# Emission by prioritised threads in a two-part transformer kernel: attention by head group, new orders of heads and projections, first recurrence blocks by token tile

## The chip, the cores and the metric

One core of one Trainium2 chip. The metric is the device time of one execution in microseconds; lower is better. Times of the kernel before: 2118.86 us, the median of 3 runs (2118.59 to 2119.57).

## What is computed

256 tokens of width 1024 pass through two models, one after the other, in float32.

```python
# first model: 4 layers, each
x = layer_norm(ALPHA * x + mixer(x))        # swa_sink, rglru, mla, swa_sink
x = layer_norm(ALPHA * x + memory_cross_attention(x))   # 4 heads of 256
x = layer_norm(ALPHA * x + conv_glu_ffn(x))             # d_ff 2816
# second model: 2 layers, each with rms_norm ahead of its parts
x = x + concat(local_heads(12 x 64), memory_heads(4 x 64)) @ w_out
x = x + conv_glu_ffn(x)
```

The mixers are: windowed attention with sinks (16 heads of 64, 4 key heads), in layers 0 and 3; a gated linear recurrence (rglru: input projection, convolution over time, two gates from 256-wide blocks, a scan over the tokens, a GELU gate, an output projection), in layer 1; latent attention (mla: down projection, norms, 8 heads of 128 + 64 rotary), in layer 2. The mixing layers of the second model are a forget-gate attention (fox) and a dilated attention, each with memory heads beside the local ones.

## The kernel before

The tokens are two tiles of 128 (t0 and t1). Every dense product is made in three matmuls of split operands: mm3 (lines 87, 88, 89) adds hi by hi, hi by lo and lo by hi, where hi is the rounded half of an operand and lo the rest. Weights come by DMA (raw, issued by SP); ScalarE casts hi (line 76) and VectorE subtracts lo (line 81), in wslot (line 66). While help_every is set, GpSimd makes each fifth lo in VectorE's place; rglru sets it, and it is reset after rglru's output projection b_w_o. The rings hold 6 raw tiles and 9 pairs of halves.

Activations are kept twice: X by rows (token on the partition), and a transposed, split pair xh, xl (or oh, ol for attention's output) that TensorE reads. The rows are turned by transposes with the identity (line 161). PSUM has three kinds of banks: four common ones (tag r) and two for each token tile.

project (line 179) runs one dense product for t0, then t1, and after each tile calls post, which takes the banks on: for the layer norm (line 227) that is VectorE's additions, statistics and scaling (lines 235 to 243), a power on GpSimd (line 224), then the transposes of X. Program text is emitted in that order, and a scheduler of the framework then orders each engine's queue by that order and by its own estimates; nobody writes a queue by hand.

attend (line 279) is called once for each token tile, when all its queries are there: it takes the heads in groups, scores (mask by identity at line 291, products at 296 and 301), the softmax (reduce 309, exp 316, scaling 325), turn (transposes of the probabilities pr, line 335, evacuated as pT), values (products with the values, line 355). It emits group i's scores, then group i-2's values, then group i-1's transposes. swa (line 431) projects keys and values, then queries of heads 0 to 7, then of 8 to 15, each for both tiles. mix (line 852) projects the forget gate and memory queries, keys, values, queries; it runs the main heads, then the memory heads of each tile.

rglru (line 477) first runs the softplus of its decay, then the gate projections gx of both tiles (transposed at 563), then conv_u (510) and gates (529) for four pairs of blocks, the transposed gate blocks (gate_bank, 560; gate_out, 573), and `late` blocks (588) whose gate projections stand near the end: late(4), gates(3), four gate_out, late(5) to late(7), four gate_out. Then b_w_o, its layer norm, and cross (line 394). There kh and kl split the memory keys (lines 400 and 401; kl on GpSimd), x_w_q projects the queries, and x_w_o the output. ffn (line 699) alternates up and down products; its order is not touched but for the lead of its first blocks.

## Time and profile before

| what | us |
|---|---|
| median of 3 runs | 2118.86 |
| the profiled execution, its own time | 2114.15 |
| its span | 2112.4 |
| TensorE busy (PE), 13528 matmuls | 2071.3 |
| VectorE busy (DVE) | 1613.5 |
| ScalarE busy (ACT) | 1218.4 |
| GpSimd busy (POOL) | 84.3 |

A window's row gives for a stretch of the span each engine's busy time and instructions, and the mean clock that was granted to TensorE (1.00 is full). A timeline's row gives start, busy time, engine, line, operation, out<-in and the number of instructions drawn together; in brackets stands how long the engine stood idle before it and what released it. Matmuls are pipelined, so a busy time is longer than the distance from one start to the next.

### The profile page before, as it was taken

How to read it: one execution, taken by the hardware profiler on the slowest of the kernel's cores; microseconds unless marked ns; L12 is line 12 of the kernel's file. 1: busy time of each engine (PE TensorE's matmuls, PEld its weight loads, DVE VectorE, ACT ScalarE, POOL GpSimd, SP SyncE). 2: the span in 40 equal slices, each digit the busy share in tenths (PEclk: the TensorE clock that was granted, in tenths of full speed). 3: DMA queues.
4: the chain of work that ended last, by engine and by line, in shares of the span. 5: the costliest groups of instructions: out<-in, count | busy, mean ns of one | idle time of the engine just before them, and what ended most of it. 6: DMA issues, size and time to landing. Idle time of an engine off the chain costs nothing.

```text
span 2112.4 us, 36195 instructions
## 1 busy us (share of the span) xinstructions
PE 2071.3 (98%) x13528; PEld 1853.0 (88%) x13528; DVE 1613.5 (76%) x3344; ACT 1218.4 (58%) x2654; POOL 84.3 (4%) x77
## 2 busy tenths in 40 slices
PE   8999999999999999999999999999999999999998
PEld 8778999887899987889997789998979998978997
DVE  6876877899787786787788778788568877677775
ACT  5545656585465554555555456665556665456563
POOL 0010000123000001000000100000000000000000
PEclk9999999999999999999999999999999999999999
DMA  8523655535455452555544347554426655524551
GB/s 331 183 94 124 228 186 183 176 102 213 168 200 187 150 188 80 180 183 192 186 152 168 120 138 251 191 179 155 160 85 220 206 182 167 183 81 170 200 180 61
DMA packets 101409, 358.23 MB, mean 170 GB/s; under 512 B 11888, under 2 KB 13552, under 8 KB 99312
## 3 DMA queue, kind: packets, MB, share of 16 engines
q1 hardware_dynamic: 101232, 355.91, 48.8%
q8 instruction: 106, 1.74, 0.3%
q14 instruction: 71, 0.58, 0.1%
HBM read 354.81 MB, written 1.05 MB: 168 GB/s over the span
## 4 chain that ended last, share of the span: by engine, by line
PE 89%; DVE 5%; ACT 3%; issue 1%; POOL 1%; DMA 1%; POOLq 0%; DVEq 0%; SPq 0%; ACTq 0%
PE bank L87 26%; PE bank L88 26%; PE bank L89 26%; PE bank L355 3%; PE bank L161 3%; DVE lo L81 2%; PE bank L335 2%; PE bank L301 1%; PE bank L296 1%; ACT pr L316 1%; ACT hi L76 1%; PE bank L291 1%; DMA row<-in_mem 0%; PE bank L769 0%; DVE nm L309 0%
## 5 line engine op out<-in xcount | busy, mean ns | idle before, releaser
L76 ACT CAST hi<-raw 128x512 fp32r<-128x512 f32 (+3 forms) x1300 | 745.9, 606 | 483.7 <-PE bank L89 222.5
L81 DVE TENSOR_TENSOR lo<-raw,hi 128x512 fp32r<-128x512 f32 (+3 forms) x1289 | 840.2, 673 | 182.3 <-ACT hi L76 177.6
L87 PE MATMUL bank<-xh,hi 128*128 128x256 f32 x1920 | 543.7, 283 | 0.0
L89 PE MATMUL bank<-xh,lo 128*128 128x256 f32 x1920 | 543.2, 283 | 0.0
L88 PE MATMUL bank<-xl,hi 128*128 128x256 f32 x1920 | 543.2, 283 | 0.0
L87 PEld LDWEIGHTS bank<-xh,hi 128*128 128x128 f32 x1920 | 368.5, 192 | 3.2 <-issue 0.2
L88 PEld LDWEIGHTS bank<-xl,hi 128*128 128x128 f32 x1920 | 368.2, 192 | 2.8
L89 PEld LDWEIGHTS bank<-xh,lo 128*128 128x128 f32 x1920 | 368.2, 192 | 0.5
L87 PE MATMUL bank<-hi,xh 128*128 128x256 f32 (+4 forms) x784 | 263.2, 336 | 0.2
L723 DVE SCALAR_TENSOR_TENSOR c<-bank,cw,c 128x254 f32<-128x254 f32 (+1 forms) x528 | 238.6, 476 | 32.1 <-ACT c L719 31.6
L89 PE MATMUL bank<-hi,xl 128*128 128x256 f32 (+4 forms) x784 | 262.1, 335 | 0.0
L88 PE MATMUL bank<-lo,xh 128*128 128x256 f32 (+4 forms) x784 | 260.4, 332 | 0.0
L87 PE MATMUL bank<-hi,gh 128*128 128x512 f32 x528 | 208.0, 394 | 0.7 <-ACT gh L92 0.7
L88 PE MATMUL bank<-lo,gh 128*128 128x512 f32 x528 | 206.9, 392 | 0.0
L89 PE MATMUL bank<-hi,gl 128*128 128x512 f32 x528 | 205.5, 390 | 0.0
L87 PEld LDWEIGHTS bank<-hi,xh 128*128 128x128 f32 x784 | 148.8, 190 | 12.0 <-ACT row L62 1.4
L89 PEld LDWEIGHTS bank<-hi,xl 128*128 128x128 f32 x784 | 148.7, 190 | 10.2 <-issue 1.0
L88 PE MATMUL bank<-lo,oh 128*128 128x512 f32 (+1 forms) x392 | 154.6, 395 | 2.8 <-DVE lo L81 1.8
L88 PEld LDWEIGHTS bank<-lo,xh 128*128 128x128 f32 x784 | 148.8, 190 | 9.3 <-issue 0.2
L87 PE MATMUL bank<-hi,oh 128*128 128x512 f32 (+1 forms) x392 | 154.4, 397 | 0.0
L89 PE MATMUL bank<-hi,ol 128*128 128x512 f32 (+1 forms) x392 | 152.7, 391 | 0.0
L719 ACT ACTIVATE c<-bank,cw 128x256 f32<-128x256 f32 x264 | 133.5, 559 | 0.2 <-PE bank L89 0.2
(270 smaller groups left out, 2570.1 us busy)
## 6 DMA issues: line engine op xcount, KB each, us to landing
raw<-in_f_w_up SPq DMA_DIRECT2D x176, 512.0 KB, 3.8
raw<-in_f_w_down SPq DMA_DIRECT2D x88, 512.0 KB, 3.8
raw<-in_m_w_up SPq DMA_DIRECT2D x88, 512.0 KB, 3.8
raw<-in_m_w_down SPq DMA_DIRECT2D x44, 512.0 KB, 3.5
raw<-in_m_w_qkv SPq DMA_DIRECT2D x48, 384.0 KB, 3.7
raw<-in_x_w_q SPq DMA_DIRECT2D x32, 512.0 KB, 3.5
raw<-in_x_w_o SPq DMA_DIRECT2D x32, 512.0 KB, 4.7
gb<-in_ln_gb SPq DMA_DIRECT2D x12, 1024.0 KB, 4.8
```

The source lines that it names most:

```text
L76: S.copy(hi[:, c], raw[:, c])
L81: eng.tensor_tensor(lo[:, c], raw[:, c], hi[:, c], ALU.subtract)
L87: T.matmul(ps, ah, bh, start=first, stop=False)
L88: T.matmul(ps, ah, bl, start=False, stop=False)
L89: T.matmul(ps, al, bh, start=False, stop=last)
L161: T.transpose(ps[:w, j * P : (j + 1) * P], b, ident)
L291: T.matmul(banks[b], l, r, start=(j == 0), stop=False)
L296: T.matmul(banks[b][:, i], l, r, start=(j == 0), stop=(j == len(pairs) - 1))
L335: T.transpose(tp[:, tile_cols(j)], prv[:, h % 2, h // 2, tile_cols(kt)], ident)
L355: T.matmul(po[i * w : (i + 1) * w, tile_cols(c - c0)], value(h0 + h, kt)[:, off : off + w], pT[h, kt], start=(kt == 0), stop=(kt == nk - 1),)
L719: S.activation(c[:, h], ps[:, h], AF.Identity, scale=cw[:, 2, b : b + 1], bias=cw[:, 3, b : b + 1])
L723: V.scalar_tensor_tensor(c[:, h, s:], ps[:, h, : 256 - s], cw[:, 2 - s, b : b + 1], c[:, h, s:], ALU.mult, ALU.add)
```

## The change

A generator (Thread) holds each piece of work, with a priority. `run` resumes the first thread in order of priority whose condition holds; a clock that is advanced by written-in costs (109 ns for a transpose, columns / 2.4 + 13.5 ns for a matmul) decides when a piece that waits for other engines may go on. So the program's text order is made by this emission, and the scheduler orders the queues from it. With it come these edits:

- project becomes `dense`, one thread for a tile, with weights that are loaded when first used (Rows); a post may yield for some microseconds before its transposes. The transposes of X go in two halves of four.
- attend makes one thread per head group; a group's scores start when its own inputs are there. swa projects in the order keys t0, first queries t0, keys t1, second queries t0, first queries t1, second queries t1, and heads 0 to 7 start when the first queries are there. mix runs the memory heads first and projects keys, queries, values.
- rglru: the two first convolution blocks are computed by token tile between the gate projections; the second late block stands ahead of gates(3); the softplus and its load move to load_constants.
- the output projections only start threads (out_proj), so that cross emits kh and kl ahead of b_w_o's weights; help_every stays set until the next ffn.
- the mask table loses a part, the latent keys' weights are laid out as four loads, and the layer norm's gains are loaded when its projection begins.

```diff
+    def run(*until, fed=False):
+        while not all(t is None or t.done or fed and t.fed for t in until):
+            soonest = None
+            for th in sorted(live, key=lambda t: t.prio):
+                r = th.when()
+                if r is None:
+                    continue
+                if r <= clk[0]:
+                    resume(th)
+                    break
+                soonest = r if soonest is None else min(r, soonest)
+            else:
+                assert soonest is not None
+                clk[0] = soonest
...
+    def transpose_rows(x, t, wait):
+        for h in range(2):
+            yield clk[0] + wait if h == 0 else again
+            again = clk[0] + 1500
+            if t == 0 and h == 0:
+                fresh("x")
+            c = slice(4 * h, 4 * h + 4)
+            transpose_split(col_blocks(x)[c], [d[:, c] for d in cur["x"]], t)
...
+    def out_proj(w, post, *heads):
+        ws = load_rows(w, D, 1)
+        for t in range(NT):
+            rows_of[t] = dense(
+                "o", ws, HALVES, t, post, need=after(*(heads[t] if heads else ())), lag=1300,
+                first=getattr(post, "prepare", None) if t == 0 else None,
+            )
...
+            yield from transpose_rows(X[:, t], t, 7500)
...
-        todo = list(range(0, heads, size))
-        made, turned = [], []
-        for i in range(len(todo) + 2):
-            if i < len(todo):
-                made.append(scores(todo[i]))
-            if i >= 2:
-                values(*turned.pop(0))
-            if 1 <= i <= len(todo):
-                turned.append(turn(*made.pop(0)))
+        def group(i, h0):
...
+            made = scores(h0)
+            recs[i].scored = clk[0]
+            turned = yield from turn(free, *made)
+            recs[i].turned = True
+            yield from values(*turned)
+            recs[i].done = True
...
+            jobs = [(0, 2, kvpost), (0, 0, qpost(0)), (1, 2, kvpost), (0, 1, qpost(1)), (1, 0, qpost(0)), (1, 1, qpost(1))]
...
+            def lead(t):
+                for a in range(2):
+                    if t == 0:
+                        ub.append((next(blocks), bank()))
+                    (hi, lo), ps = ub[a]
+                    xth, xtl = cur["x"]
+                    for k in range(KD):
+                        x = tile_cols(t)
+                        mm3(ps[:, x], hi[:, k], lo[:, k], xth[:, k, x], xtl[:, k, x], k == 0, k == KD - 1)
+                        yield
...
             late(ng)
+            late(ng + 1)
             gates(3, *prev)
             for c in range(ng):
                 gate_out(c, gz[:, c])
-            for c in range(ng + 1, KD):
+            for c in range(ng + 2, KD):
                 late(c)
...
-        project_full(cur["o"], A["b_w_o"], post)
-        help_every[0] = 0
+        out_proj(A["b_w_o"], post)
...
+            help_every[0] = 0
+            pinned[0] = "f"
+            run(*[spawn(lead(t), need=r) for t, r in enumerate(rows_ready())])
...
-            for w, f in ((1, kpost), (2, vpost), (0, qpost)):
-                project(cur["x"], load_rows(A["m_w_qkv"][l, w], 768, 1), halves, f)
+            for w, f in ((1, kpost), (0, qpost), (2, vpost)):
+                ws = load_rows(A["m_w_qkv"][l, w], 768, 1)
```

In the first local attention, TensorE's order before, from the first group's transposes of probabilities (ident,pr) to the products with the values (pT,vv); hi,xl, hi,xh and lo,xh are projections:

```order
L335 MATMUL bank<-ident,pr 128x128 x2
L87 MATMUL bank<-hi,xh 128x512
L88 MATMUL bank<-lo,xh 128x512
L335 MATMUL bank<-ident,pr 128x128 x3
L89 MATMUL bank<-hi,xl 128x512
L335 MATMUL bank<-ident,pr 128x128
L355 MATMUL bank<-pT,vv 64x128 x8
L335 MATMUL bank<-ident,pr 128x128 x8
L355 MATMUL bank<-pT,vv 64x128 x8
```

And the same place after the change, from the second four transposes of that group on:

```order
L532 MATMUL bank<-ident,pr 128x128 x4
L161 MATMUL bank<-hi,xh 128x512
L162 MATMUL bank<-lo,xh 128x512
L163 MATMUL bank<-hi,xl 128x512
L266 MATMUL bank<-ident,q 128x128 x4
L560 MATMUL bank<-pT,vv 64x128 x8
L161 MATMUL bank<-hi,xh 128x512
L162 MATMUL bank<-lo,xh 128x512
L163 MATMUL bank<-hi,xl 128x512
L481 MATMUL bank<-maskh,identr 128x512 x2
L491 MATMUL bank<-kT,qT 128x128 x8
```

Before, the transposes and products of two groups followed each other with three projection matmuls among them; now three matmuls and four transposes of q stand between a group's transposes and its products, and the next group's scores come after.

At the recurrence's entry, TensorE's order before (ident,X are the layer norm's transposes, ident,gx those of the first gate projection):

```order
L88 MATMUL bank<-lo,xh 128x512
L89 MATMUL bank<-hi,xl 128x512
L161 MATMUL bank<-ident,X 128x128 x4
L563 MATMUL bank<-ident,gx 128x128 x2
L161 MATMUL bank<-ident,X 128x128 x4
L87 MATMUL bank<-hi,xh 128x512
```

And now (xh,hi of 128x128 are the first convolution blocks for tile t0):

```order
L163 MATMUL bank<-xh,lo 128x128
L161 MATMUL bank<-xh,hi 128x128
L162 MATMUL bank<-xl,hi 128x128
L163 MATMUL bank<-xh,lo 128x128
L266 MATMUL bank<-ident,X 128x128 x4
L161 MATMUL bank<-xh,hi 128x128
L162 MATMUL bank<-xl,hi 128x128
L163 MATMUL bank<-xh,lo 128x128
```

33 such matmuls stand before the first four transposes of X, and 15 between these and the second four; the transposes of gx have moved behind t1's blocks.

GpSimd's queue from the recurrence to the layer norm behind the cross attention, before (gz belongs to the gates, lo to weights, kl to the memory keys, rs is the power of a norm):

```order
L81 TENSOR_TENSOR lo<-raw,hi 128x512 x5
L574 TENSOR_TENSOR gz<-gz,u 128x256 x4
L81 TENSOR_TENSOR lo<-raw,hi 128x512 x3
L401 TENSOR_TENSOR kl<-memkv,kh 128x512 x4
L224 TENSOR_TENSOR rs<-rs,mhalf 128x1 x10
```

And now:

```order
L89 TENSOR_TENSOR lo<-raw,hi 128x512 x5
L834 TENSOR_TENSOR gz<-gz,u 128x256 x4
L89 TENSOR_TENSOR lo<-raw,hi 128x512 x2
L634 TENSOR_TENSOR kl<-memkv,kh 128x512 x4
L89 TENSOR_TENSOR lo<-raw,hi 128x512 x3
L400 TENSOR_TENSOR rs<-rs,mhalf 128x1
L89 TENSOR_TENSOR lo<-raw,hi 128x512
L400 TENSOR_TENSOR rs<-rs,mhalf 128x1
L89 TENSOR_TENSOR lo<-raw,hi 128x512 x3
L400 TENSOR_TENSOR rs<-rs,mhalf 128x1 x8
```

The last low half of b_w_o stands behind the four kl instead of ahead of them, and six further halves, of the cross attention's weights, are among the powers.

## Rows read from the trace of the kernel before

**Rows 1.** Page, part 1: busy time, share of the span, instructions.

```profile
PE 2071.3 (98%) x13528; PEld 1853.0 (88%) x13528; DVE 1613.5 (76%) x3344; ACT 1218.4 (58%) x2654; POOL 84.3 (4%) x77
```

**Rows 2.** Windows by stage: stretch, length, busy time of each engine, granted clock, DMA.

```profile
86.00:129.00 43.00, 40.13 (x263) 27.36 (x262) 32.46 (x116) 23.88 (x95) 0.00 (x0) 0.96 0.15 50
388.00:416.00 28.00, 25.21 (x114) 20.25 (x113) 25.07 (x46) 14.57 (x26) 6.56 (x6) 0.94 0.52 187
410.00:416.00 6.00, 5.92 (x25) 4.86 (x26) 4.28 (x14) 2.17 (x4) 0.30 (x1) 0.72 0.76 283
452.00:457.00 5.00, 2.19 (x18) 2.02 (x18) 5.00 (x12) 4.12 (x8) 1.74 (x2) 1.00 0.00 0
472.00:500.00 28.00, 23.81 (x103) 17.94 (x103) 27.51 (x51) 20.17 (x40) 15.34 (x7) 1.00 0.53 188
744.00:801.00 57.00, 55.23 (x307) 47.20 (x306) 48.73 (x122) 34.90 (x87) 3.92 (x6) 1.00 0.60 202
801.00:824.00 23.00, 20.51 (x109) 15.49 (x108) 16.54 (x51) 10.40 (x33) 0.00 (x0) 0.85 0.32 115
1140.00:1165.00 25.00, 22.58 (x147) 14.36 (x145) 20.84 (x74) 18.31 (x69) 0.00 (x0) 1.00 0.13 44
1440.00:1490.00 50.00, 48.47 (x307) 44.23 (x306) 39.84 (x118) 25.80 (x62) 3.32 (x4) 1.00 0.46 148
1520.00:1570.00 50.00, 48.63 (x351) 38.19 (x351) 35.29 (x91) 31.79 (x100) 0.00 (x0) 1.00 0.28 95
1570.00:1600.00 30.00, 29.03 (x169) 25.15 (x168) 18.65 (x32) 13.88 (x28) 1.42 (x2) 1.00 0.39 141
1840.00:1896.00 56.00, 54.16 (x358) 41.81 (x357) 42.55 (x109) 31.57 (x97) 0.00 (x0) 1.00 0.34 121
1896.00:1925.00 29.00, 28.04 (x168) 23.90 (x169) 18.71 (x33) 14.52 (x30) 1.42 (x2) 1.00 0.41 145
```

**Rows 3.** Waits of TensorE over the span: us, times, longest.

```profile
PE bank L161 <- DVE X L243: 4.3, 4, 1.9
PE bank L335 <- DVE pr L325: 3.4, 6, 1.5
PE bank L87 <- ACT gz L570: 2.8, 1, 2.8
...
PE bank L161 <- DVE cn L634: 1.2, 2, 0.7
```

**Rows 4.** Timeline of TensorE, first local attention.

```profile
94.24 0.27 PE L335 MATMUL bank<-ident,pr 128*128 128x128 f32 x1
94.63 0.43 PE L355 MATMUL bank<-pT,vv 128*64 128x128 f32 x2
96.17 1.09 PE L355 MATMUL bank<-pT,vv 128*64 128x128 f32 x14 [1.11 <-ACT pT L62]
```

**Rows 5.** Timeline of TensorE, 128-column matmuls with weights of their own, first mixing layer.

```profile
1523.11 1.00 PE L301 MATMUL bank<-cT,sel 128*128 128x128 f32 x8
1524.04 0.49 PE L301 MATMUL bank<-kv,qT 64*128 64x128 f32 x4
```

**Rows 6.** Timeline of TensorE, last gates of the recurrence.

```profile
456.83 0.36 PE L87 MATMUL bank<-uh,hi 128*128 128x256 f32 x1 [2.81 <-ACT gz L570]
```

**Rows 7.** Timeline of GpSimd, output projection of the recurrence.

```profile
475.38 1.30 POOL L81 TENSOR_TENSOR lo<-raw,hi 128x512 fp32r<-128x512 f32 x1 [5.12 <-ACT hi L76]
480.06 6.68 POOL L81 TENSOR_TENSOR lo<-raw,hi 128x512 fp32r<-128x512 f32 x1 [3.37 <-ACT hi L76]
486.70 6.41 POOL L401 TENSOR_TENSOR kl<-memkv,kh 128x512 fp32r<-128x512 f32 x4
493.80 0.99 POOL L224 TENSOR_TENSOR rs<-rs,mhalf 128x1 f32<-128x1 f32 x1 [0.69 <-DVE rs L223]
```

**Rows 8.** Timeline of VectorE, the same place.

```profile
479.51 6.09 DVE L81 TENSOR_TENSOR lo<-raw,hi 128x512 fp32r<-128x512 f32 x10
```

**Rows 9.** Timeline of TensorE, the same place.

```profile
486.79 0.50 PE L88 MATMUL bank<-lo,oh 128*128 128x512 f32 x1 [1.02 <-POOL lo L81]
```

More of the change, by code (lines that the diff above doesn't have):

```diff
@@ L2 @@
 from contextlib import ExitStack
+from collections import deque
 from itertools import chain
@@ L84, in wslot, with pe, __init__, when @@
         return res
+    clk = [0.0]
+    live = []
+    born = [0]
+    pinned = [None]
+    def pe(ins):
+        if pinned[0] in CFG["pin"]:
+            tc.keep_in_program_order(ins)
+    class Thread:
+        def __init__(self, gen, prio, need, lag):
+            self.gen, self.prio, self.ready, self.lag = gen, prio, need, lag
+            self.done, self.end, self.fed = False, None, False
+        def when(self):
+            r = self.ready() if callable(self.ready) else self.ready
+            return r
+    def spawn(gen, prio=None, need=0.0, lag=0.0):
+        born[0] += 1
+        th = Thread(gen, 100 + born[0] if prio is None else prio, need, lag)
+        live.append(th)
+        return th
+    def after(*ths):
+        def f():
+            if all(t is None or t.done for t in ths):
+                return max([t.end for t in ths if t is not None] + [0.0])
+            return None
+        return f
+    def both(*needs):
+        def f():
+            got = [n() if callable(n) else n for n in needs]
+            return None if None in got else max(got)
+        return f
+    def resume(th):
+        now[0] = th
+        try:
+            r = next(th.gen)
+            th.ready = 0.0 if r is None else r
+        except StopIteration:
+            th.done, th.end = True, clk[0] + th.lag
+            live.remove(th)
+    now = [None]
+    def run(*until, fed=False):
[12 more added lines that the diff above has]
+                clk[0] = soonest
     def mm3(ps, ah, al, bh, bl, first, last):
-        T.matmul(ps, ah, bh, start=first, stop=False)
-        T.matmul(ps, ah, bl, start=False, stop=False)
-        T.matmul(ps, al, bh, start=False, stop=last)
+        clk[0] += 3 * (ps.shape[-1] / 2.4 + 13.5)
+        pe(T.matmul(ps, ah, bh, start=first, stop=False))
+        pe(T.matmul(ps, ah, bl, start=False, stop=False))
+        pe(T.matmul(ps, al, bh, start=False, stop=last))
     def split(hi, lo, src):
@@ L177, in col_blocks, with dense, gen @@
         return [x[:, i * P : (i + 1) * P] for i in range(n)]
-    def project(src, ws, cols, post, nk=KD):
-        for t in range(NT):
+    opened = [0, 0]
+    def dense(src, ws, cols, t, post, nk=KD, need=0.0, lag=0.0, first=None):
+        def gen():
+            th = now[0]
+            yield ws.fits
+            if first:
+                first()
+            if isinstance(src, str):
+                readers[src].append(th)
+            h, l = cur[src] if isinstance(src, str) else src
             banks = []
+            opened[t] += 1
             for c0, c1 in cols:
@@ L216, in by_block, with rows_ready @@
+    def rows_ready():
+        return [after(r) for r in rows_of]
     def by_block(w):
@@ L502, in gpost @@
                 gx.append(z)
-            project(cur["x"], gw, [(0, ng * P)], gpost)
+            def lead(t):
[7 more added lines that the diff above has]
+                        mm3(ps[:, x], hi[:, k], lo[:, k], xth[:, k, x], xtl[:, k, x], k == 0, k == KD - 1)
+                        yield
+            ub, ready = [], rows_ready()
+            pinned[0] = "b"
+            parts = []
+            for t in range(NT):
+                parts.append(dense("x", gw, [(0, ng * P)], t, gpost, need=ready[t]))
+                parts.append(spawn(lead(t), need=both(ready[t], after(*parts[-1:] if t == 0 else parts[1:]))))
+            run(*parts)
+            pinned[0] = None
+            oth, otl = fresh("o")
+            xth, xtl = cur["x"]
             def block_mm(ps, hi, lo):
@@ L745, in ffn @@
             nh = CFG["head"]
-            first = [wslot(wup[j], [1024, 1024]) for j in range(nh)]
+            first = []
             def row():
@@ L751, in ffn, with lead @@
             hx = [row().rearrange("p (j c) -> p j c", c=256) for _ in range(NT)]
-            for t in range(NT):
+            def lead(t):
+                xth, xtl = cur["x"]
                 for j0 in range(0, nh, 2):
@@ L823, in add @@
                 V.tensor_tensor(X[:, t, half(h)], X[:, t, half(h)], ps[h], ALU.add)
[L825 to L829 removed]
+            yield from then(t, row or (lambda: ph.tile([P, D], F32, tag="xn", name="xn", bufs=1)), add)
         return post
```

495 lines of the change are left out of this document (327 added, 168 removed).

## The prediction, before the result was known

> **What bounds the kernel now.** I read the page first: TensorE is busy for 2071.3 of 2112.4 us [rows 1]. So no engine but TensorE can set the time, and there are only 2112.4 - 2071.3 = 41.1 us in which it stands still. A change that leaves its matmuls as they are can gain these 41 us at most, and what a lower clock costs besides. The total of columns is unchanged here (48 matmuls of 256 become 96 of 128, below), so the whole question is which of the 41 us go and what new ones come.
>
> Next come the windows, cut by stage [rows 2]. For each stage two numbers are to be seen: its length less the PE column (idle), and (1 - clock) times its length (what the slow clock took: the granted clock falls to its half level, 1.2 GHz, behind some of the stops, and its mean shows it). Feed forward stages, which are most of the program, have next to nothing of either and keep their order. The idle time sits in the stages that the change reorders: first local attention 43.00 - 40.13 = 2.87 idle and 0.04 x 43 = 1.72 of clock; second local attention 25.00 - 22.58 = 2.42; latent attention 1.77 + 2.49 idle and 0.15 x 23 = 3.45 of clock; first mixing layer 1.53 + 1.37 + 0.97 = 3.87; second 1.84 + 0.96 = 2.80. Together 21.4 us. The recurrence has 2.79 idle and 0.28 x 6 = 1.68 of clock at its entry, 2.81 idle before its last gates, and 4.19 in its output projection.
>
> Then the waits say what TensorE stood for [rows 3]: the layer norm's X (4.3 us in 4 waits), the softmax's pr (3.4 in 6), gz (2.8, once), cn (1.2 in 2). These are chains of small operations on VectorE and ScalarE whose result TensorE asks for too early. They are cured by other matmuls in between, and that is what an order can give.
>
> **What the change does, and its price.** Against the profiled execution's own 2114.15 us, term by term:
>
> 1. Attention by threads. In the first local attention, TensorE issued the last transpose of pr at 94.24, two of the products with the values, and then stood 1.11 us for pT until 96.17 [rows 4]. Now projections stand between scores, transposes and products, as the order shows at this very place: after the first group's last four transposes come three projection matmuls and four transposes of q before the first product. With a 512-column matmul at twice the 256-column one's 0.122 us of term 4, and a transpose at the 0.116 of a 128-column one there, that is 3 x 0.24 + 4 x 0.116 = 1.2 us, against 96.17 - 94.24 = 1.93 us that the result took; so 0.7 us and its refilling (term 2), about 1.1, stay of 4.6: **-3.5**. The second local attention has the same order: -2.0 of 2.42. In latent attention the first tile's scores still stand together, and about 18 matmuls separate them from the transposes of pr; I let the cn waits (1.2) and some four waits of pr at their mean (3.4 / 6 = 0.57) stay, 3.4 in all: -4.3 of 7.7. In the mixing layers memory heads now run inside the key projections and the main heads' scores between queries and values; I leave about a third: -2.4 and -2.2. Sum **-14.4**; ends 0 (every wait moves) and -21.4.
>
> 2. Refilling. A stop costs more than its idle time: the two products before 96.17 need 2 x 1.09 / 14 = 0.16 us and could have been over at 94.79, but the next began 1.38 us later, with 1.11 shown as idle [rows 4]. That is some 0.2 us for each stop. Of the 13 waits for X, pr, cn and pT at these places I let eight go: **-1.6** (0 to -2.6).
>
> 3. Layer norms. Transposes of X now stand 36 matmuls behind the first tile's projection, not 18. Of the four waits for X, 1.9 is at the recurrence's entry and 1.4 in the following cross attention (both counted there); the rest is **-1.0** (0 to -1.0).
>
> 4. Recurrence, entry. 48 matmuls of the two first convolution blocks now stand between the gate projections and the transposes of X. They fill the 1.9 us wait and, with it, the slow stretch after it: **-3.7** of 4.47 (0 to -4.5). But these blocks are computed by token tile: 96 matmuls of 128 columns take the place of 48 of 256. A 256-column one takes 2.19 / 18 = 0.122 us [rows 2] (window 452 to 457). For 128 columns with weights of their own the nearest row is cT by sel: eight from 1523.11 to 1524.04, 0.116 us each [rows 5]; so half the columns take nearly the same time. 96 x 0.116 - 48 x 0.122 = **+5.3**. The lower end is half price, 0.061 us each, which adds nothing. I take the row, since weights change with every matmul in both.
>
> 5. Recurrence, last gates. TensorE waits 2.81 us for the last gates' input until 456.83 [rows 6]; the trace puts it on ScalarE's gz, and VectorE is busy for all 5.00 us there [rows 2]. Now a second late block, 24 matmuls x 0.122 = 2.9 us, stands ahead of the gates and covers it. But VectorE's chain is no shorter, and the block is missing behind the gates, where the output projection waits for the same chain: **-1.0** (0 to -2.8).
>
> 6. Output projection of the recurrence and the cross attention behind it. GpSimd makes each fifth low half of the weights, and now goes on doing so for the queries and output of this cross attention: six halves more. Its queue is in a new order, too: the four kl now stand ahead of a half of the output projection, and later halves ahead of the layer norm's power. Such a half takes 1.30 us, but 6.68 us from 480.06 [rows 7], which is while VectorE ran ten subtractions of its own, 479.51 to 485.60 [rows 8]; it ended 1.1 us after they did. TensorE paid 1.02 us for that [rows 9]. Behind kl (6.41 us for four) the same half may come 6.4 us later, or no later if kl run in GpSimd's idle 5.12 and 3.37 us before those halves: -1.0 to +6.4, I take +1.8, nearer to the idle side, since kl depend on nothing of this layer. The six new halves: 0 to 6 x (6.68 - 1.30) = 32 us; they are loaded well ahead of their use, so I take +0.9. The power (0.99 us) behind three halves may come 3.9 us later and X's wait of 1.4 there may go: -1.4 to +3.9, I take 0. Together **+2.7**.
>
> The Trainium skill (page "SBUF — State Buffer", section "SBUF: two separate sides") says that VectorE and GpSimd share one pair of ports as an exclusive lock, and that a VectorE operation with two SBUF inputs shuts out a GpSimd operation that reads SBUF for the whole instruction. By that rule each half that meets a burst of VectorE's subtractions waits for the burst, as the row at 480.06 agrees; if every half met one, the time would be that of the slower rival below.
>
> 7. Start. The softplus of the recurrence, its load and two activations move to the load of constants, beside the first weights, where TensorE is short of operands. Two small operations of the power's 0.99 us bound what is exposed: 0 to +2.0, **+0.7**. Its place in the recurrence was hidden. The smaller mask, four loads for two of the latent keys, and the earlier load of the norm's gains cost nothing: the DMA share of the attention stages is 0.60 or less [rows 2].
>
> Sum: -14.4 - 1.6 - 1.0 - 3.7 + 5.3 - 1.0 + 2.7 + 0.7 = **-13.0**: 2101.15 us of that execution. The median of the runs shown lies 2118.86 - 2114.15 = 4.71 higher, so **2105.9**.
>
> **Rivals.** (a) *The waits only move.* The softmax chain is as long as it was, and new places ask for it: two thirds of terms 1 and 2 stay, +9.6 and +1.1, so -2.3 and 2116.6. For it: some distances stay short (1.2 us against 1.93 above; the latent scores). Against it: VectorE and ScalarE are far from full in these stages (32.46 and 23.88 of 43 us), and the order shows matmuls in nearly all the gaps. 0.17.
> (b) *Slower: GpSimd starves.* Seven halves stand behind kl or in the new queue, and each that VectorE shuts out as at 480.06 costs 5.4 us if TensorE waits for all of it. Five of them: 27 us in place of term 6, -15.7 + 27 = +11.3, 2130.2. It decides from four on ((15.7 + 4.2) / 5.4 = 3.7). For it: the row at 480.06. Against it: TensorE paid only 1.02 of the 5.4 there, and halves at 475.38 went in 1.30 with VectorE at work. 0.12.
> (c) *All of it goes.* Terms at their best ends: -21.4 - 2.6 - 1.0 - 4.5 + 0 - 2.8 - 2.4 + 0 = -34.7, 2084.2. Against it: short distances as in (a), and the price of 128 columns. 0.08.
> That the change doesn't do what it says is no rival: the compiled order shows it.
>
> **How the numbers follow.** The forecast itself has 0.63, with a range of its own from 2099 to 2113. The range of 8 in 10 takes in (a) and the ends of terms 4 and 6, and leaves out (b) and (c): 2093 to 2121. What a measurement can tell from no change is 0.2%, 4.2 us, so faster is below 2114.6 and slower above 2123.1. Faster: 0.61 of the forecast, 0.06 of (a), 0.08 of (c) = 0.75. Same: 0.02 + 0.09 of (a) + 0.02 of (b) = 0.13. Slower: 0.02 of (a) + 0.10 of (b) = 0.12.
>
> **What would show it.** TensorE's idle total falls from 41 to about 27 us while its matmuls grow by 48. In the windows of the five attention stages idle and clock together fall from 21 to about 7 us. The two convolution blocks' 96 matmuls stand about 0.116 us apart. The wait for gz is gone, with VectorE's chain named a little later. GpSimd's halves in the cross attention after the recurrence take 1.3 us. Wrong it is if pr and pT still lead the list of waits with several us, if the clock is halved in new stretches, or if TensorE waits for GpSimd's lo by more than 3 us.

## The result and the profile after

The changed kernel takes 2079.48 us (median of 4 runs, 2077.86 to 2080.38) against 2118.73 (2112.78 to 2119.57, 4 runs): ratio 0.9828, 95% interval 0.9811 to 0.9845. Forecast were 2105.9 and a range from 2093. The direction was right; the gain is three times the forecast and below the range.

The page of the changed kernel, part 1:

```profile
PE 2039.4 (98%) x13576; PEld 1850.5 (89%) x13576; DVE 1612.3 (78%) x3340; ACT 1214.3 (58%) x2656; POOL 97.7 (5%) x83
```

The span fell by 2112.4 - 2076.1 = 36.3 us. TensorE's idle time fell only from 41.1 to 36.7. The other 31.9 us left its *busy* column (2071.3 in [rows 1]), although 48 matmuls were added. The prediction had looked for the whole gain in the idle time.

Where it happened, by windows (columns as in [rows 2]). The five attention stages before the change: local, latent, local, first and second mixing layer:

```profile
54.30:147.30 93.00, 90.12 (x493) 68.29 (x492) 72.37 (x189) 51.71 (x147) 6.04 (x5) 0.98 0.34 118
752.50:852.40 99.90, 95.64 (x523) 79.43 (x522) 75.42 (x192) 54.31 (x138) 9.27 (x10) 0.97 0.41 140
1106.70:1200.00 93.30, 90.87 (x501) 68.31 (x500) 76.36 (x198) 50.90 (x143) 6.88 (x6) 1.00 0.37 128
1456.70:1589.70 133.00, 130.04 (x843) 114.63 (x842) 90.77 (x239) 74.26 (x194) 2.08 (x3) 1.00 0.44 148
1784.70:1914.70 130.00, 127.23 (x813) 110.85 (x812) 90.67 (x206) 67.46 (x176) 1.40 (x2) 1.00 0.43 143
```

The same stages in the changed kernel:

```profile
58.20:141.60 83.40, 83.13 (x493) 65.30 (x492) 69.69 (x185) 49.92 (x144) 6.02 (x5) 1.00 0.40 143
750.10:842.60 92.50, 89.24 (x523) 77.76 (x522) 73.78 (x191) 54.04 (x138) 9.24 (x10) 1.00 0.44 152
1095.40:1180.00 84.60, 84.05 (x501) 66.14 (x500) 75.01 (x197) 50.47 (x143) 6.94 (x6) 1.00 0.38 136
1435.20:1562.60 127.40, 125.11 (x843) 113.36 (x842) 89.71 (x239) 72.75 (x195) 2.08 (x3) 1.00 0.46 155
1756.60:1879.20 122.60, 121.06 (x814) 109.14 (x813) 91.37 (x207) 66.78 (x177) 1.28 (x2) 1.00 0.47 151
```

Together 549.2 became 510.5: -38.7 us, with the same matmuls. Idle time is 7.4 of it (15.3 to 7.9); the PE column is 31.3, and the half clock is part of that. In the local stages next to nothing is idle now, and the clock stays at 1.00, where 0.02 x 93 + 0.03 x 99.9 = 4.9 us had gone to its half level.

What a busy column can hide is seen in the timeline of TensorE. Before the change, second local attention (a float32 matmul leaves two records, so x2 is one score of a head over 256 keys, on 64 of the array's rows):

```profile
1153.69 0.70 PE L301 MATMUL bank<-kT,qT 64*128 64x256 f32 x2
1154.31 0.55 PE L335 MATMUL bank<-ident,pr 128*128 128x128 f32 x3
1154.79 0.70 PE L301 MATMUL bank<-kT,qT 64*128 64x256 f32 x2
1155.42 0.33 PE L335 MATMUL bank<-ident,pr 128*128 128x128 f32 x1
1155.67 0.70 PE L301 MATMUL bank<-kT,qT 64*128 64x256 f32 x2
1156.30 0.43 PE L355 MATMUL bank<-pT,vv 128*64 128x128 f32 x2
1156.66 0.70 PE L301 MATMUL bank<-kT,qT 64*128 64x256 f32 x2
```

And in the changed kernel, the same four scores:

```profile
1137.17 1.13 PE L491 MATMUL bank<-kT,qT 64*128 64x256 f32 x8
1138.24 0.50 PE L161 MATMUL bank<-hi,xh 128*128 128x512 f32 x1
```

Alone, a score holds TensorE for 1154.31 - 1153.69 = 0.62 us, and none of it shows as idle. Four in one run, on the upper and the lower half of the rows in turn, take 1138.24 - 1137.17 = 1.07 us, 0.27 each. The compiled order says how often this happens. A half-array matmul is one that uses 64 of the array's rows or 64 of its columns. TensorE's queue changed between full array, half the rows and half the columns 171 times before, and 102 times now; of 344 half-array matmuls 89 stood without a neighbour on the other half, now 40. From start to next start the half-array matmuls of the five stages took 82.3 us before and take 60.6 now. Of these 21.7 us, 3.1 are idle time behind them and some 2.1 the half clock; 16.4 are neither. The full-array matmuls of the five stages fell by 9.9 us that are neither, 6.2 of them in the transposes of pr, which stood beside the broken runs (worked out from the starts, idle times and clock in the traces).

Not everything got better. The table gives each stage from the start of its first projection to the next stage's, in us, worked out from the starts in the traces (all else up to TensorE's last matmul); half-array is a part of the five attention stages, and e1 to e14 are the experiments below.

| stage | before | changed | e1 | e2 | e3 | e4 | e13 | e14 |
|---|---|---|---|---|---|---|---|---|
| start | 54.3 | 58.2 | 59.3 | 58.3 | 58.0 | 57.1 | 55.3 | 54.4 |
| local attention, first | 93.1 | 83.4 | 88.9 | 90.2 | 83.4 | 87.0 | 88.8 | 82.2 |
| recurrence | 94.5 | 101.6 | 103.3 | 103.2 | 103.1 | 104.3 | 94.5 | 94.6 |
| its cross attention | 64.4 | 63.5 | 63.7 | 63.5 | 63.5 | 63.5 | 64.4 | 62.7 |
| latent attention | 100.0 | 92.6 | 94.0 | 92.5 | 92.5 | 93.2 | 100.0 | 92.5 |
| local attention, second | 93.3 | 84.6 | 90.1 | 99.1 | 85.1 | 89.6 | 91.3 | 83.4 |
| mixing, first | 133.1 | 127.5 | 146.6 | 127.5 | 129.7 | 130.9 | 130.5 | 126.7 |
| mixing, second | 130.1 | 122.5 | 129.8 | 122.6 | 127.1 | 125.4 | 126.7 | 122.1 |
| all else | 1342.6 | 1335.1 | 1342.5 | 1335.2 | 1335.3 | 1335.5 | 1342.3 | 1335.7 |
| half-array | 82.3 | 60.6 | 79.4 | 77.7 | 66.8 | 73.8 | 69.9 | 57.1 |

The recurrence lost 7.1 us and the start 3.9. TensorE's waits in the changed kernel (us, times, longest):

```profile
PE bank L161 <- ACT hi L84: 8.7, 4, 6.4
PE bank L162 <- POOL lo L89: 5.9, 3, 2.6
PE bank L161 <- ACT gz L830: 3.4, 1, 3.4
...
PE bank L532 <- DVE pr L520: 1.0, 2, 0.6
```

Against [rows 3]: pr fell from 3.4 to 1.0, and X and cn no longer stand among the larger waits, as forecast. The wait that the profile puts on gz grew from 2.8 to 3.4 (e8 below shows what it is for), and GpSimd's lo leads the waits of the recurrence.

Two of the prediction's three signs of being wrong came: TensorE waits 5.9 us for GpSimd's lo, and the granted clock is halved in new stretches, behind two stops of the recurrence. At the same work (456 to 463 and 486 to 492 us) the kernel before had 1.00:

```profile
449.00:456.00 7.00, 6.00 (x38) 6.04 (x39) 6.49 (x19) 5.66 (x15) 3.60 (x1) 0.76 0.22 77
477.00:483.00 6.00, 5.14 (x16) 4.07 (x17) 6.00 (x4) 3.46 (x7) 6.00 (x5) 0.72 0.55 186
```

### The profile page after: what moved, and what is told of

Same layout as the page of the kernel before. It is cut to its first block, busy times and chain, and to the rows that moved or that the text cites. A ratio compares the mean times of both kernels' runs of the same rounds, so it can differ in the third digit from the quotient of the medians.

```text
span 2076.1 us, 36278 instructions
## 1 busy us (share of the span) xinstructions
PE 2039.4 (98%) x13576; PEld 1850.5 (89%) x13576; DVE 1612.3 (78%) x3340; ACT 1214.3 (58%) x2656; POOL 97.7 (5%) x83
## 4 chain that ended last, share of the span: by engine, by line
PE 68%; DVE 5%; ACT 2%; issue 1%; DMA 1%; POOL 0%; POOLq 0%; DVEq 0%; SPq 0%; ACTq 0%
PE bank L161 20%; PE bank L163 20%; PE bank L162 20%; DVE lo L89 2%; PE bank L560 2%; PE bank L266 2%; PE bank L491 1%; PE bank L532 1%; PE bank L486 1%; ACT hi L84 1%; ACT pr L511 0%; PE bank L481 0%; DMA row<-in_mem 0%; DVE nm L504 0%; DVE X L424 0%
## 5 line engine op out<-in xcount | busy, mean ns | idle before, releaser
L89 DVE TENSOR_TENSOR lo<-raw,hi 128x512 fp32r<-128x512 f32 (+2 forms) x1283 | 840.1, 678 | 188.2 <-ACT hi L84 184.3
L161 PE MATMUL bank<-xh,hi 128*128 128x256 f32 (+1 forms) x1936 | 548.3, 283 | 3.4 <-ACT gz L830 3.4
L163 PE MATMUL bank<-xh,lo 128*128 128x256 f32 (+1 forms) x1936 | 548.2, 283 | 0.0
L162 PE MATMUL bank<-xl,hi 128*128 128x256 f32 (+1 forms) x1936 | 548.0, 283 | 0.0
L161 PE MATMUL bank<-hi,xh 128*128 128x256 f32 (+4 forms) x784 | 267.8, 342 | 0.1
L977 DVE SCALAR_TENSOR_TENSOR c<-bank,cw,c 128x254 f32<-128x254 f32 (+1 forms) x528 | 238.8, 477 | 31.7 <-ACT c L973 31.3
L161 PE MATMUL bank<-hi,oh 128*128 128x512 f32 (+1 forms) x392 | 158.9, 407 | 2.3 <-ACT hi L84 2.3
```

The costliest lines, as they stand in the source:

```text
L89: eng.tensor_tensor(lo[:, c], raw[:, c], hi[:, c], ALU.subtract)
L161: pe(T.matmul(ps, ah, bh, start=first, stop=False))
L162: pe(T.matmul(ps, ah, bl, start=False, stop=False))
L163: pe(T.matmul(ps, al, bh, start=False, stop=last))
L977: V.scalar_tensor_tensor(c[:, h, s:], ps[:, h, : 256 - s], cw[:, 2 - s, b : b + 1], c[:, h, s:], ALU.mult, ALU.add)
```

## The experiments

The first four are about the attention stages. Theory P: unbroken runs of half-array matmuls with projections between them. Rivals: the orders as such (O), or long waits alone (W).

**e1, the emission's clock off** (the clock of `run`, not TensorE's).

```diff
-            return r
+            return None if r is None else 0.0
```

> The changed kernel with the emission's clock off: every thread may go on as soon as its inputs are emitted, so a head group's scores, transposes and products are emitted one behind the other, and only the new order of heads, keys, queries and values is left. As compiled, TensorE's queue then changes 166 times between full-array and half-array matmuls (before 171, changed kernel 102), and 86 of 344 half-array matmuls stand alone (89; 40). Theory P (the gain came from unbroken runs of half-array matmuls with projections between the runs, which the clock makes): the five attention stages give back 20 to 35 of their 39 us, own time 2098 to 2113. Rival O (the new orders of heads and projections carry the gain, whatever the emission): within 8 us of the changed kernel, below 2086.

Measured: 2127.14 us, beside 2111.42 for the kernel before on that chip. Rival O falls, and P's range was too small: without the emission's clock the change is a loss. The half-array matmuls went back to 79.4 us, and all else gave back its 7.5 us too, so these belong to the emission's clock as well. Waits are longer again:

```profile
PE bank L1192 <- issue: 7.2, 1, 7.2
PE bank L266 <- DVE X L424: 6.4, 4, 3.4
```

The first is one stop in the first mixing layer, before 1482.77. The waits give no cause, but the timeline does: the forget gate's product needs sp, and VectorE ends the last copy of it just then:

```profile
1482.50 0.17 DVE L1186 COPY sp<-sp 128x12 f32<-128x12 f32 x1
```

In the changed kernel that product is held back by 6 us of the emission's clock (`yield clk[0] + 6000`), and other matmuls stand there. The stop makes much of the 19 us that this stage lost beyond the changed kernel; a granted clock of 0.94 over 1467 to 1614 us makes more of it.

**e2, local attention's old order.**

```diff
-            jobs = [(0, 2, kvpost), (0, 0, qpost(0)), (1, 2, kvpost), (0, 1, qpost(1)), (1, 0, qpost(0)), (1, 1, qpost(1))]
+            jobs = [(0, 2, kvpost), (1, 2, kvpost), (0, 0, qpost(0)), (1, 0, qpost(0)), (0, 1, qpost(1)), (1, 1, qpost(1))]
...
-                    return after(m[2], m[h0 // 8])
+                    return after(m[2], m[0], m[1])
```

> The changed kernel with local attention's old order: keys of both tiles, first queries of both, second queries of both, and no head starts before all queries of its tile. As compiled, 136 changes between full and half array and 67 lone half-array matmuls. Theory P: about half of the way back in these two stages (34 of 69 changes), so 7 to 11 of their 18.6 us, own time 2085 to 2089. Rival W (the part that half-heads bring is the long waits alone): at most the idle time that these stages lost, 2.6 and 1.9 us, own time below 2083.

Measured: 2100.88 us; the two stages grew by 6.8 and 14.5, twice what P said and far beyond W. The second is worse than before the change. Windows show why the size was missed, the whole stage and a part of it: the granted clock.

```profile
1103.00:1203.00 100.00, 96.13 (x506) 71.68 (x505) 77.21 (x198) 51.70 (x145) 6.94 (x6) 0.93 0.35 117
1149.00:1163.00 14.00, 14.00 (x45) 7.60 (x44) 5.81 (x25) 5.47 (x25) 0.00 (x0) 0.51 0.12 39
```

0.07 x 100 = 7 us went to the half level here, all of them shown as busy. Of the 21.3 us some 8 are half-array time that is neither idle nor half clock, which is P's size; 5 are idle time and 7 the clock. So starting heads 0 to 7 with the first queries does both here: it fills waits and keeps the clock up.

**e3, the mixing layers' old order** (keys, values, queries; the call for the memory heads moved behind the main heads).

```diff
-            for w, f in ((1, kpost), (0, qpost), (2, vpost)):
+            for w, f in ((1, kpost), (2, vpost), (0, qpost)):
```

> The changed kernel with the mixing layers' old order: keys, values, queries, and the memory heads behind the main heads of each tile. As compiled, 116 changes between full and half array and 53 lone half-array matmuls (changed kernel 102 and 40). Theory P: 14 of 31 changes come back, so 3 to 6 of these stages' 12.9 us, own time 2081 to 2084. Rival O (this order is what made the two stages faster): 10 us or more, own time above 2087.

Measured: 2086.58 us, the two stages +2.2 and +4.5, half-array time +6.2. That is 6.7 of their 13.1 us: a little more than P gave, less than O. About half of these two stages' gain is the order's.

**e4, halves one behind the other.**

```diff
-            terms = {(i, b): score(h0 + 2 * i + b) for i in range(g) for b in range(2)}
+            terms = {(i, b): score(h0 + 2 * i + b) for b in range(2) for i in range(g)}
...
-                for c in range(c0, c0 + nc_):
-                    for i in range(per):
+                for i in range(per):
+                    for c in range(c0, c0 + nc_):
```

> The changed kernel with one thing altered inside the runs: the heads of one array half first, then those of the other, in scores and in products with the values, in place of turns between the halves. Matmuls, their number, the groups and what stands between them stay. Theory P (a run of half-array matmuls is cheap because neighbours on different halves run side by side: 0.11 us from start to start in the trace for a 128-column one, 0.22 on the same half): 344 half-array matmuls of which most lose a partner, about 0.1 us each, +20 to +45 us, own time 2098 to 2123. Rival W (only waits on other engines matter): within 4 us of the changed kernel.

Measured: 2095.49 us, and the attention stages +15.6, half-array time +13.2. W falls; P's mechanism holds, but below its range of +20 to +45: 0.1 us for each of the 344 was too much. One run of eight scores (16 records) in the second local attention, in e4:

```profile
1121.11 1.71 PE L491 MATMUL bank<-kT,qT 64*128 64x128 f32 x16
1122.75 0.50 PE L161 MATMUL bank<-hi,xh 128*128 128x512 f32 x1
```

and in the changed kernel:

```profile
1128.36 1.16 PE L491 MATMUL bank<-kT,qT 64*128 64x128 f32 x16
1129.45 0.50 PE L161 MATMUL bank<-hi,xh 128*128 128x512 f32 x1
```

1.64 us against 1.09. The Trainium skill (page "TensorE: Matmul & The Clock Gate", section "Part 3: Packing small matmuls — row/col tiling") says that matmuls at different places of the array run at the same time; these rows agree.

**e13, the kernel before with its runs kept.** One line of the kernel before; nothing of the change is in it.

```diff
-                    for i in range(per):
+                    for i in reversed(range(per)):
```

> The kernel before, with one thing altered: in the products with the values, of each pair of heads the second stands first, so that a run's first product needs the transposed probabilities that are finished last, and the run is not begun before all of it can go. As compiled, TensorE's queue changes 134 times between full and half array (before 171, changed kernel 102), and 59 half-array matmuls stand alone (89 and 40). Nothing else of the change is in it. Theory P (broken runs of half-array matmuls are a large part of the gain): 6 to 12 us faster than the kernel before, all of it in the five attention stages and the cross attentions unchanged. Rival W (the gain came from projections that fill the waits, and a run that starts later only waits longer): within 3 us, or slower.

Measured: 2103.31 us against 2111.72 for the kernel before on that chip, ratio 0.9957 (0.9943 to 0.9971): 8.4 to 9 us, inside P's range. Half-array time fell from 82.3 to 69.9 while the rest of these stages stayed. Its page shows the gain in the busy column, as the change's own: 2071.3 became

```profile
PE 2059.0 (98%) x13528; PEld 1846.5 (88%) x13528; DVE 1613.3 (77%) x3344; ACT 1216.8 (58%) x2654; POOL 84.2 (4%) x77
```

So 12.4 of the 21.7 us of half-array time can be had without any projection between the groups.

The next ones are about what was lost.

**e5, whole blocks.** The threads of lead are dropped and conv_u makes its two blocks itself.

```diff
-                parts.append(spawn(lead(t), need=both(ready[t], after(*parts[-1:] if t == 0 else parts[1:]))))
...
-                    if hblk == 0:
-                        ps = ub[a][1]
-                    else:
-                        hi, lo = next(blocks)
-                        ps = bank()
-                        block_mm(ps, hi, lo)
+                    hi, lo = next(blocks)
+                    ps = bank()
+                    block_mm(ps, hi, lo)
```

> The changed kernel with the first two convolution blocks whole again: 48 matmuls of 256 columns behind the gate projections, not 96 of 128 among them. Theory A (128 columns cost 0.111 us against 0.120 for 256, so the split is a loss of 96 x 0.111 - 48 x 0.120 = 4.9 us and nothing else covers it): the recurrence, 101.6 us in the changed kernel, falls by 4 to 5. Rival F (the split fills the wait for the layer norm's X and the slow clock behind it, 2.1 and 1.7 us in the kernel before): it falls by 1.5 or less, or not at all.

Measured: 2081.26 us, recurrence 103.3, within what it took in e1 to e4. F holds: the price of the split is real, its gain is as large. The wait for X is back in e5:

```profile
401.90 0.33 PE L819 MATMUL bank<-ident,gx 128*128 128x128 f32 x1 [0.68 <-ACT gx L63]
...
404.34 0.66 PE L266 MATMUL bank<-ident,X 128*128 128x128 f32 x4 [2.12 <-DVE X L424]
```

**e6, no help from GpSimd** from the recurrence's output projection on.

```diff
+        help_every[0] = 0
         out_proj(A["b_w_o"], post)
```

> The changed kernel without GpSimd's help from the recurrence's output projection on: VectorE makes those low halves, in the output projection and in the cross attention behind it. Theory S (TensorE waits for halves that GpSimd makes too late, 5.9 us in three waits, one of them starved for 6.34 us and one behind the four kl): the recurrence falls by 4 to 6 us, the cross attention stays. Rival V (VectorE is full there, 1.3 us of its time for a half more are missing on its own chain): the recurrence stays within 1.5 us or grows.

Measured: 2075.58 us; recurrence 99.4 and its cross attention 62.1, together 3.6 less than in the changed kernel's first profile and 4.7 less than in its second (e10: 103.2 and 63.0). That is S's size and not V's, but the recurrence alone fell by 2.2 or 3.8, not 4 to 6. In the changed kernel GpSimd did this:

```profile
471.46 6.34 POOL L89 TENSOR_TENSOR lo<-raw,hi 128x512 fp32r<-128x512 f32 x1 [4.01 <-ACT hi L84]
477.76 6.80 POOL L634 TENSOR_TENSOR kl<-memkv,kh 128x512 fp32r<-128x512 f32 x4
484.53 2.95 POOL L89 TENSOR_TENSOR lo<-raw,hi 128x512 fp32r<-128x512 f32 x2
```

VectorE made eight halves of its own beside the first:

```profile
471.45 1.28 DVE L89 TENSOR_TENSOR lo<-raw,hi 128x512 fp32r<-128x512 f32 x2
...
472.98 3.69 DVE L89 TENSOR_TENSOR lo<-raw,hi 128x512 fp32r<-128x512 f32 x6
```

and TensorE waited for both halves, at 477.8 for the starved one and at 486.0 for the one behind kl:

```profile
477.86 0.50 PE L162 MATMUL bank<-lo,oh 128*128 128x512 f32 x1 [2.63 <-POOL lo L89]
486.29 0.50 PE L162 MATMUL bank<-lo,oh 128*128 128x512 f32 x1 [2.46 <-POOL lo L89]
```

In e6 the second wait is gone. The first is not, since VectorE makes that half as late:

```profile
473.50 0.50 PE L162 MATMUL bank<-lo,oh 128*128 128x512 f32 x1 [2.89 <-DVE lo L89]
```

From the stop before the last gates to the 41st of the output projection's 96 matmuls the changed kernel takes 27.9 us and e6 28.2; from there to the last, 17.9 and 13.8. So S is right for the half behind kl; the starved half cost no more than the same half on VectorE, as V had it.

**e7, the memory values' weights ahead.**

```diff
-        project_full(cur["o"], A["mem_w_v"], post)
+        ws = load_rows(A["mem_w_v"], D, 1)
+        for k in range(KD):
+            ws[k]
+        project(cur["o"], ws, HALVES, post)
```

> The changed kernel with the eight weight tiles of the memory values asked for at once, ahead of the loads that follow, as the kernel before does. The changed kernel's start is 3.9 us longer than before, with TensorE waiting on ScalarE's casts at 37.1, 42.6 and 47.1 us, which wait for these tiles. Theory L (the lazy loads put them late in the DMA queue): the start falls from 58.2 to 54 to 55 us. Rival M (the softplus and the load of its parameters, moved here, keep VectorE, ScalarE and the queue busy): the start stays above 57 us.

Measured: 2080.09 us and a start of 58.2: L falls. SP's queue in the changed kernel showed another cause:

```profile
14.64 0.33 SPq L78 DMA_DIRECT2D raw<-in_mem_w_v  x1
25.10 0.33 SPq L254 DMA_DIRECT2D mst<-in_c_mask  x1
```

and SP's waits put 9.3 us of that on the end of the softplus (sp):

```profile
SPq L254 <- DVE sp L246: 9.3, 1, 9.3
```

**e9, softplus back.** Its load and its operations return from load_constants to the recurrence.

```diff
-        nc.sync.dma_start(bp, A["b_par"])
-        with phase("initb") as ph:
-            e = ph.tile([P, 3, KD], F32, tag="e", name="e", bufs=1)
-            softplus_neg(sp[:, 0], bp[:, 7], e)
```

> The changed kernel with the softplus of the decay, its load and scalings back at the recurrence's start. In the changed kernel's trace SP issues nothing from 14.64 to 25.10 us: the next in its queue is the mask's load, which went out at 11.98 before the change, and behind it stand the weights of the memory values. Theory Q (the mask's buffer takes the place of the softplus's scratch, so its load waits for the softplus, and SP's queue with it): the mask's load goes out near 12 us again and the start falls from 58 to 54 to 55 us, own time 3 to 4 us shorter than the unchanged one on the same chip. Rival M (VectorE and ScalarE are the bound at the start anyway): the start stays above 57.

Measured: 2076.91 us, 3.5 less than the changed kernel's 2080.39 (e10) on that chip; the start is 55.1, and the mask's load goes out early:

```profile
10.10 0.33 SPq L247 DMA_DIRECT2D mst<-in_c_mask  x1
```

Q holds: a load that waited for a scratch buffer held up SP's queue for ten microseconds, and the weights behind it.

**e8, the late block back.**

```diff
-            late(ng + 1)
             gates(3, *prev)
...
-            for c in range(ng + 2, KD):
+            for c in range(ng + 1, KD):
```

> The changed kernel with the second late block behind the last gates again, as before. It did not take the wait away (3.53 us beyond the pace before the last gates, 2.97 before the change). Theory C (the wait is for a chain of VectorE and ScalarE that takes the same time wherever the block stands): the wait before the gates grows by about 2.9 us, and the same time is saved behind them, the recurrence within 1 us of 101.6. Rival B (the block hides 2.9 us of the chain, which is longer in the changed kernel for another reason): the recurrence grows by 2 to 3 us.

Measured: 2076.63 us, recurrence 100.1, some 3 less than in e2 to e4 (1.5 less than in the changed kernel's first profile). Neither B nor C. In e8 the wait stands before the gates,

```profile
449.04 0.47 DVE L781 SCALAR_TENSOR_TENSOR u<-bank,bp,u 128x253 f32<-128x253 f32 x1
449.65 0.35 PE L161 MATMUL bank<-uh,hi 128*128 128x256 f32 x1 [3.38 <-ACT gz L830]
```

and in the changed kernel, as long, before the second late block (xh,hi), with the gates (uh,hi) behind it:

```profile
449.38 0.47 DVE L781 SCALAR_TENSOR_TENSOR u<-bank,bp,u 128x253 f32<-128x253 f32 x1
450.00 0.35 PE L161 MATMUL bank<-xh,hi 128*128 128x256 f32 x1 [3.37 <-ACT gz L830]
...
454.12 0.41 PE L161 MATMUL bank<-uh,hi 128*128 128x256 f32 x1
```

Neither the block nor the gates read gz. The four common banks go round in turn, and what comes next after the first late block gets the bank of the last convolution block, which VectorE (L781) still reads. As compiled, the first matmul behind the wait waits for that very operation in the kernel before, in the changed one and in e8, and in each it starts 0.15 us after its end. So the second late block could not fill the wait: it needs the same bank, and puts the gates off by its own 4.1 us, some of it at half clock. Without it TensorE's waits for low halves in the output projection are 4.8 us (0.83 and 3.94), with it 7.4 (0.84, 1.43, 2.63 and 2.46).

**e10, the changed kernel again**, beside e11 and e12.

> The changed kernel unaltered, timed on the same chip as the two versions below. Both theories: 2079 us and 0.982 of the kernel before, within 3 us.

Measured: 2080.39 us (2079.4 to 2080.9), ratio 0.9835 (0.9816 to 0.9853).

**e11, three repairs**: the edits of e6, e8 and e9 together.

> The changed kernel with three parts undone: the softplus back at the recurrence (e9), the second late block behind the last gates (e8), no help of GpSimd from the recurrence's output projection on (e6). Theory R (the three losses stand in different places and add up): start -3.5, recurrence and cross attention -4.6 for the help and -2.9 for the block, so 10 to 11 us less than the changed kernel of the same chip, 2068 to 2070. Rival D (help and block both serve the same chain of VectorE, which gives back one of them): 6 to 8 us less.

Measured: 2070.04 us (2069.55 to 2070.49), 10.35 less than e10: R. They add up.

**e12, and whole blocks**: e11 with the edit of e5.

> The three repairs and the first two convolution blocks whole (e5). In e5 the recurrence came out alike either way: 4.9 us of matmul time were saved and came back as waits, for X and for GpSimd's halves. Theory R (with GpSimd's waits gone, the part of the saving that those took remains): 2 to 3 us less than the three repairs alone. Rival F (the wait for X and VectorE's chain take it all): within 1 us.

Measured: 2069.1 us (2068.81 to 2069.39), 0.9 less than e11: F. The split is worth nothing to within 1 us.

**e14, and strict turns.** e12 with the products with the values in this order:

```diff
-                    for i in range(per):
...
-                        for kt in range(nk):
+                    for kt in range(nk):
+                        for i in reversed(range(per)):
```

> The version of e12 (three repairs, whole blocks) with products with the values in strict turns between the array's halves, key tile outside, head inside, second head first. As compiled, 92 changes between full and half array and none of the 344 half-array matmuls alone (102 and 40). Theory P: the ends of the runs, 0.1 us for each of 40, and 10 changes at about 0.1 us: 3 to 6 us less than e12, 2063 to 2066, all in the five attention stages. Rival W: within 1.5 us of e12.

Measured on another chip: 2066.2 us (2063.26 to 2067.12), ratio 0.9781 (0.9767 to 0.9795). Its attention stages are 3.7 less than the changed kernel's, all but 0.2 in half-array matmuls, and 3.4 less than e12's (510.4 to 507.0): P, at its low end. This version is below both kernels; against e12, which ran elsewhere, the medians (2.9 less) agree.

**e15, only the second head first**: e12 with the line of e13.

> The version of e12 with the second head of a pair first in the products with the values, and the key tiles inside as before: 92 changes between full and half array, 32 half-array matmuls alone. Theory P (both changes of shape and lone matmuls cost): between e12 and e14. Rival S (only the changes of shape cost): like e14.

Measured: 2063.15 us in its one run, beside 2063.26 of e14's profiled execution; half-array time 57.9 and 57.1. In e12 half-array time is 60.6, so 2.7 of the 3.4 us come with ten changes of shape and eight lone matmuls fewer, and 0.7 with the other 32. That is nearer to S: here the changes of shape cost more; the order inside a run adds little once it takes turns. That turns themselves are worth having, e4 showed.

## Why the prediction was wrong

**The step that failed is where the gain can come from (first paragraph).** It says that there are only 41.1 us in which TensorE stands still, and that such a change "can gain these 41 us at most, and what a lower clock costs besides". As a number this held, but not its ground: 31.9 of the 36.3 us came out of busy time, and the clock is only a small part of that. The busy time of one matmul is longer than its pace (283 ns mean for a 256-column one whose start to start is 0.12), so short stops and the price of a lone half-array matmul hide in it. The sum over start-to-start distances, which term 2 touched with 0.2 us for each stop, was the view to use throughout.

**Terms 1 and 2** gave -16.0 for the five stages, with -24.0 as the end of their range; they measured -38.7. The long waits went as forecast: idle and clock together fell from 20.2 to 7.9 us, where 21 to 7 had been said. Missing was a term for broken runs of half-array matmuls, put at nothing without a reason: -16.4 in these matmuls and -9.9 in the full-array ones, which are neither idle nor clock. The compiled order had it: scores and products in broken pairs before, whole runs now. It was read for distances between producer and user only. (The two records at 94.63 in [rows 4] are one product, not two; the sum is the same.)

**Term 3** gave -1.0; all else fell by 7.5, 1.4 of it in each of the three other cross attentions. e1 gives all of it back, so it comes of the emission's clock; idle time makes only 2.0 of it (3.6 to 1.6), and which of that clock's waits brings the rest is open.

**Term 4** gave +1.6 for the entry, and its size was nearly right. The price was right: 96 matmuls at 0.111 us, for instance

```profile
400.00 0.27 PE L163 MATMUL bank<-xh,lo 128*128 128x128 f32 x1
400.12 0.27 PE L161 MATMUL bank<-xh,hi 128*128 128x128 f32 x1
```

where 0.116 was taken; the wait for X went, too. e5 and e12 put the whole at 0 to +0.9.

**Term 5** gave -1.0: wrong in sign; undoing it gained some 3 us (e8). The wait was taken for the gates' input, on the word of the releaser that the trace names. It is for a PSUM bank, which the second late block needs just as well, so the block stands behind the wait and not in it.

**Term 6** gave +2.7. The place was right: the half starved at 480.06 in [rows 7] starves again at 471.46, and the half behind kl comes late as rival (b) had it. The waits measure 2.6 and 2.5 us of idle time, and taking the help away gains some 4 to 5 (e6), all of it behind the first. Rival (b)'s extent did not come: three halves were waited for (0.84, 2.63 and 2.46 us), not five at 5.4.

**Term 7** gave +0.7, bounded at 2.0; it was +3.9. The working priced the softplus's operations, and not the load that waits for its scratch buffer and what stands behind it on SP (e9).

**Rival (a)** did not come about, but e1 shows what it rested on: with the emission's clock off the waits do move, and the kernel is slower than before. **Rival (c)** had 2084.2, near the result, by luck: its sum has every wait gone and no loss, and neither is so.

## What to carry to other kernels

Cost a reordering by start-to-start distances, not by an engine's idle column. In the compiled order look for two things beside the distance from producer to user: how often the queue changes between full-array and half-array matmuls, and whether neighbours on the half array use different halves; e13 gained 0.4% with one line. A step that moves "to where it is hidden" takes its scratch buffer along: ask which load waits for that buffer, and what is queued behind the load. Work that is to fill a wait must not need what the wait is for: look for the bank as well as for the operands.

## What the runs showed of the hardware

- A float32 score of 64 rows by 256 keys holds TensorE for 0.62 us alone and 0.27 us in a run of four that takes turns between the halves. Eight of 128 keys take 1.09 us in turns and 1.64 one half behind the other.
- The granted clock's fall to its half level took 4.9 us from two of the attention stages before and none there after; a reordering alone (e2) brought it to 0.93 over 100 us of a stage that had 1.00 in the kernel before.
- A low half on GpSimd took 1.4 to 1.7 us in most places and 6.34 beside eight of VectorE's own subtractions, as 6.68 beside ten in [rows 7] and [rows 8].
- The profile put three waits of 2.8 to 3.4 us on ScalarE's gz (kernel before, changed kernel, e8) that were for a PSUM bank: the last read of it, on VectorE, ended 0.15 us before TensorE went on, each time.
